# Down projection of a two-layer decoder trunk: seven products of half blocks in two phases

## The chip, the cores and the metric

One core of a Trainium2 chip runs the whole kernel. The metric is the device time of one execution in microseconds (us). TensorE (PE) multiplies, and PEld is its loading of the stationary operand; VectorE (DVE) and ScalarE (ACT) work element by element; GpSimd (POOL) does small steps and issues some transfers; SyncE (SP) issues most transfers. Sixteen DMA engines, shared by all queues, move the data.

## The reference

Two layers, each a token mixer and a gated feed-forward part with a short causal convolution, on 512 tokens of width 1024. The change lies in the last line of the feed-forward part:

```python
D_MODEL, SEQ, DEPTH, D_FF, FFN_CONV = 1024, 512, 2, 2816, 3

def conv_ffn(h, w_up, ffn_conv_w, w_down):
    u = causal_dwconv(h @ w_up, ffn_conv_w)
    gate, val = u[..., :D_FF], u[..., D_FF:]
    return (jax.nn.silu(gate) * val) @ w_down

for l in range(DEPTH):
    ...
    h = rmsnorm(x, g_pre_ffn[l])
    y = conv_ffn(h, w_up[l], ffn_conv_w[l], w_down[l])
    x = x + rmsnorm(y, g_post_ffn[l])
```

## The kernel before

**Arithmetic.** Every float32 operand of a large product is held as two tiles: a rounded part (format float32r) and the remainder. `mm3` (line 115) adds three products into one accumulator: rounded x rounded, rounded x remainder, remainder x rounded. `wsplit` (lines 99 to 108) loads a 512 KB weight tile `raw` over SyncE's queue (L102), ScalarE copies it into the rounded part (L105), VectorE subtracts that to get the remainder (L107). `split_evac` (L120, L121) does the same for a value on the chip.

**Up projection.** Lines 759 to 797 go over 22 pairs of channel blocks, gate block j = i and value block j = i + 22. Each block is 24 products of 512 tokens. `conv3` empties its accumulator: ScalarE takes one tap (L646), VectorE adds two (L648). Then comes the gate (L790, ScalarE), the product of the two (L791, VectorE), and the split into `G[0]` and `G[1]` (L120, L121), the transposed left side of the down projection: channels on the partitions, tokens along the tile, two blocks (k2) to a tile.

**Down projection.** Lines 800 to 832: 2816 channels are 22 blocks in 11 steps k2, the 1024 output columns two halves `hf`, the 512 tokens four row tiles `c`. For each half, step and row tile `down` does 2 x 3 products of 128 tokens by 512 columns. Half 0 adds up in four accumulators `acc`, half 1 in four `aux`. The weights of the last NTAIL = 5 steps of half 1 are made early and kept in the large pool `gp`, so that the end can go row tile by row tile: 30 products of tile c, then `postnorm` of c (square sums on ScalarE, L198; product with the gain, L200, and residual, L207, on VectorE; root on GpSimd, L203 and L204). Between the layers, `prenorm_a` of the next layer follows (L166, L175), `prenorm_b` transposes the result on TensorE (L183) and splits it (L188, L190), and `head` starts the next layer's products. After the last layer the rows go out (L209).

**Room and order.** `gp` has 21 tiles of 4 KB a partition, `wp` 6 for weights, `rp` 3 for raw tiles, `wk` 10 work tiles; each kind of accumulator has 4 banks. The program places instructions by dependencies, priority of program order and free tiles; a pool's tiles go to their first writers in program order. On the chip every engine and queue runs its own instructions strictly in that order and waits only on semaphores: where a load stands late in the program, it still starts as soon as its queue gets to it and its tile is free.

## Time and profile before

| | us |
|---|---|
| median of 3 runs (lowest, highest) | 1130.92 (1129.97, 1133.09) |
| the profiled execution | 1130.86 |
| its span, first to last instruction | 1129.1 |
| TensorE busy (products) | 1108.7, 98% |
| VectorE busy | 659.4, 58% |
| ScalarE busy | 455.9, 40% |
| DMA moved | 111.07 MB, mean 98 GB/s |

The profile is one execution. "Busy" is the time in which an engine had an instruction in work. Products overlap, so the mean time of one (0.389 us for 512 columns) is longer than the pace at which they follow each other; the pace is a stretch divided by its count. The layers' down projections lie at about 449 to 569 and 1007 to 1123 us. A wait is put down to what ended it last.

### The profile page before, as it was taken

What the parts mean: (1) busy time and instruction counts of PE and PEld (TensorE: products, weight loads), DVE (VectorE), ACT (ScalarE), POOL (GpSimd) and SP (SyncE); (2) the same over time, 40 slices, a digit from 0 to 9 for tenths busy, and PEclk for the clock granted to TensorE, in tenths of its full rate; (3) what the DMA queues carried; (4) which work ended last, traced back from release to release, by engine and by line L of the source; (5) the groups of instructions that cost most, each with busy time, mean ns of one, the idle gap of its engine ahead of it and who ended that gap; (6) DMA issues with size and microseconds to landing.
All of it is one profiled execution on the core that took longest, in us unless ns stands there. A gap on an engine that the chain in (4) does not pass through costs nothing.

```text
span 1129.1 us, 14371 instructions
## 1 busy us (share of the span) xinstructions
PE 1108.7 (98%) x5504; PEld 921.1 (82%) x5504; DVE 659.4 (58%) x1094; ACT 455.9 (40%) x882; POOL 46.7 (4%) x106
## 2 busy tenths in 40 slices
PE   6999999999999999999999999999999999999997
PEld 6877788988888888888897777889888888888886
DVE  5588775566666565223557887566566655652223
ACT  5454563444334443223354445444443334431221
POOL 2000011100000000000100000110000000000001
PEclk9999999999999999999999999999999999999999
DMA  7331440233333332334223215202222333233322
GB/s 265 110 98 45 145 135 13 89 112 93 95 101 104 93 93 93 98 108 127 81 93 107 77 62 187 75 19 90 98 94 93 96 102 102 94 93 93 97 90 74
DMA packets 33171, 111.07 MB, mean 98 GB/s; under 512 B 4192, under 2 KB 4352, under 8 KB 33104
## 3 DMA queue, kind: packets, MB, share of 16 engines
q1 hardware_dynamic: 29808, 102.98, 28.7%
q0 software_dynamic: 1232, 4.04, 1.1%
q10 hardware_dynamic: 2064, 3.15, 1.0%
q8 instruction: 43, 0.70, 0.3%
q14 instruction: 24, 0.20, 0.1%
HBM read 104.91 MB, written 2.10 MB: 95 GB/s over the span
## 4 chain that ended last, share of the span: by engine, by line
PE 91%; DVE 2%; DMA 1%; ACT 1%; issue 0%; ACTq 0%; DVEq 0%; POOLq 0%; POOL 0%
PE acc L115 74%; PE aux L115 11%; PE aux L513 1%; DMA wk<-wk 1%; PE aux L183 1%; PE aux L470 1%; PE aux L569 1%; PE aux L499 1%; PE aux L549 0%; DVE wk L412 0%; DVE w L107 0%; DMA raw<-in_wout_dram 0%; ACT wk L484 0%; PE aux L605 0%; PE aux L627 0%
## 5 line engine op out<-in xcount | busy, mean ns | idle before, releaser
L115 PE MATMUL acc<-g,w 128*128 128x512 f32 (+1 forms) x2256 | 482.0, 376 | 0.0
L115 PEld LDWEIGHTS acc<-g,w 128*128 128x128 f32 x2256 | 404.2, 188 | 76.7
L107 DVE TENSOR_TENSOR w<-raw,w 128x1024 fp32r<-128x1024 f32 (+2 forms) x162 | 192.8, 1191 | 267.6 <-ACT w L105 267.5
L105 ACT ACTIVATE w<-raw 128x1024 fp32r<-128x1024 f32 (+2 forms) x162 | 167.7, 1035 | 336.9 <-PE acc L115 294.7
L115 PE MATMUL acc<-w,h 128*128 128x384 f32 (+2 forms) x672 | 146.1, 364 | 0.7 <-DVE h L190 0.5
L648 DVE SCALAR_TENSOR_TENSOR wk<-acc,par,wk 128x511 f32<-128x511 f32 (+1 forms) x176 | 131.3, 746 | 3.0
L115 PEld LDWEIGHTS acc<-w,h 128*128 128x128 f32 x672 | 118.7, 190 | 17.2 <-issue 4.8
L115 PE MATMUL acc<-h,w 128*128 128x512 f32 x432 | 106.4, 398 | 0.0
L115 PEld LDWEIGHTS acc<-h,w 128*128 128x128 f32 x432 | 78.9, 188 | 18.2 <-issue 1.5
L115 PE MATMUL acc<-w,g 128*128 128x512 f32 x384 | 88.7, 389 | 0.0
L115 PEld LDWEIGHTS acc<-w,g 128*128 128x128 f32 x384 | 72.1, 188 | 15.0
L646 ACT ACTIVATE wk<-acc,par 128x512 f32<-128x512 f32 x88 | 58.9, 669 | 0.0
L115 PE MATMUL aux<-g,g 128*128 128x512 f32 x240 | 55.0, 389 | 0.0
L120 ACT ACTIVATE g<-wk 128x512 fp32r<-128x512 f32 x36 | 22.8, 633 | 76.3 <-DVE wk L791 68.3
L115 PEld LDWEIGHTS aux<-g,g 128*128 128x128 f32 x240 | 45.0, 188 | 9.3
L115 PE MATMUL acc<-h,g 128*128 128x512 f32 x192 | 45.2, 393 | 0.1
L115 PE MATMUL aux<-w,h 128*128 128x512 f32 x192 | 43.8, 389 | 0.0
L115 PEld LDWEIGHTS aux<-w,h 128*128 128x128 f32 x192 | 36.0, 188 | 7.5
L115 PEld LDWEIGHTS acc<-h,g 128*128 128x128 f32 x192 | 35.6, 188 | 7.7 <-ACT g L120 0.5
L175 DVE SCALAR_TENSOR_TENSOR wk<-x,rs,gb 128x512 f32<-128x512 f32 x32 | 22.7, 748 | 29.4 <-POOL rs L170 29.4
L203 POOL TENSOR_SCALAR rs<-ss 128x1 f32<-128x1 f32 x16 | 5.7, 358 | 747.0 <-ACT junk L198 747.0
L121 DVE TENSOR_TENSOR g<-wk,g 128x512 fp32r<-128x512 f32 x36 | 24.9, 690 | 18.6 <-ACT g L120 18.6
(172 smaller groups left out, 934.3 us busy)
## 6 DMA issues: line engine op xcount, KB each, us to landing
raw<-in_wup_dram SPq DMA_DIRECT2D x88, 512.0 KB, 3.5
raw<-in_wdn_dram SPq DMA_DIRECT2D x44, 512.0 KB, 3.5
raw<-in_wch_dram SPq DMA_DIRECT2D x18, 512.0 KB, 4.2
raw<-in_wout_dram SPq DMA_DIRECT2D x16, 512.0 KB, 3.6
raw<-in_wtb_dram SPq DMA_DIRECT2D x16, 384.0 KB, 3.0
raw<-in_wta_dram SPq DMA_DIRECT2D x8, 392.0 KB, 4.4
wk<-wk ACTq DMA_DIRECT2D x40, 64.0 KB, 2.1
x<-in_x_dram SPq DMA_DIRECT2D x4, 512.0 KB, 7.3
```

Source lines behind the costliest of these rows:

```text
L105: i = nc.scalar.activation(hi[:, :n], raw[:, :n], AF.Copy)
L107: after(nc.vector.tensor_tensor(lo[:, :n], raw[:, :n], hi[:, :n].bitcast(F32), ALU.subtract), gate2)
L115: i = nc.tensor.matmul(o, ls[a], rs[b], start=first and n == 0, stop=last and n == 2)
L120: i = nc.scalar.activation(hi, ps, AF.Copy)
L121: return i, nc.vector.tensor_tensor(lo, ps, hi.bitcast(F32), ALU.subtract)
L175: st[c] = nc.vector.scalar_tensor_tensor(h[:, :512], xs[c][:, sl], rs, gb[:, sl], ALU.mult, ALU.mult)
L183: nc.tensor.transpose(ps[:, k * 128:(k + 1) * 128], hs[hf][:, k * 128:(k + 1) * 128], ident)
L470: i = nc.tensor.matmul(pss[p][:, pr, k0:256], q[kv][r, qs], k[r, ks], start=n == 0, stop=n == 2)
L499: nc.tensor.transpose(ps[:, g * 128:(g + 1) * 128], t.P[:, g], ident)
L513: y.lastpv = nc.tensor.matmul(aos[k][64 * p:64 * p + 64, o:o + 256], y.avt[:, t.b - 1 + kh, t.kv * 64:t.kv * 64 + 64], t.PT[:, kh * 512 + ...
L646: nc.scalar.activation(u[:, :512], ps, AF.Copy, scale=cw[:, 2:3])
L648: nc.vector.scalar_tensor_tensor(u[:, d:512], ps[:, 0:512 - d], cw[:, 2 - d:3 - d], u[:, d:512], ALU.mult, ALU.add)
```

## The change

The down projection is seen as a product of 2 x 2 half blocks: the left side A has token halves (rows 0 to 255, 256 to 511) and even and odd channel blocks, the right side B has even and odd channel blocks and column halves. Instead of eight products of half blocks it uses seven, of sums of the blocks (Winograd's form). Per step k2 that is 7 products x 2 row tiles x 3 terms.

- `forms`, called once per pair of channel blocks in the up projection, makes the left sums on VectorE and splits them. Four left sides (products 1, 4, 5, 6) stay in `G`. Those of products 3 and 7 (tile X, 512 KB) and 2 (tile Y, 256 KB) are stored to DRAM by three transfers on GpSimd's queue.
- Phase one does products 1, 5, 6, 4 for all 11 steps, with all eight accumulators; a step loads two 512 KB weight tiles, makes three right sums (VectorE) and four splits. The last two steps are done together, product by product.
- Then three work tiles take combinations: `s1` = product 1, `sE` = product 5 less (1 + 6), `sF` = (1 + 6) + product 4.
- Phase two does products 2, 3, 7, with six accumulators. It loads the weights again (512 and 256 KB a step), makes one right sum and three splits, and loads X and Y back on GpSimd's queue. The last 4 steps are done row tile by row tile: row tiles 0 and 1 from products 2 and 3, row tiles 2 and 3 from product 7, with two more VectorE sums each before `postnorm`.

```diff
@@
-NTAIL = 5
+NTAIL = 4
@@
+    dp = ctx.enter_context(tc.tile_pool(name="dp", bufs=1, space=bass.MemoryType.DRAM))
@@
+    def forms(G, D7, k2, e, o):
+        for a in range(2):
+            G[a][k2] = slot(F32R, hp if k2 < 4 else gp)
+        g0, g1 = G[0][k2], G[1][k2]
+        a11, a21, a12, a22 = e[:, 0:256], e[:, 256:512], o[:, 0:256], o[:, 256:512]
+        t, u = work(), work()
+        nc.vector.tensor_tensor(t[:, 0:256], a21, a22, ALU.subtract)
+        nc.vector.tensor_tensor(t[:, 256:512], t[:, 0:256], a11, ALU.subtract)
+        nc.vector.tensor_tensor(u[:, 0:256], a12, t[:, 256:512], ALU.add)
+        nc.vector.tensor_tensor(u[:, 256:512], a11, a21, ALU.subtract)
+        split_evac(a11, g0[:, 0:256], g1[:, 0:256])
+        split_evac(a22, g0[:, 256:512], g1[:, 256:512])
+        _, last = split_evac(t[:, 0:512], g0[:, 512:1024], g1[:, 512:1024])
+        uh, ul, y = work(F32R), work(F32R), work(F32R)
+        split_evac(u[:, 0:512], uh[:, 0:512], ul[:, 0:512])
+        split_evac(a12, y[:, 0:256], y[:, 256:512])
+        D7[0][k2] = dp.tile([128, 1024], F32R, tag=f"dx{k2}", name=nm("dx"))
+        if k2 % 2 == 0:
+            D7[1][k2] = dp.tile([128, 1024 if k2 + 1 < NK2 else 512], F32R, tag=f"dy{k2}", name=nm("dy"))
+        else:
+            D7[1][k2] = D7[1][k2 - 1]
+        nc.gpsimd.dma_start(D7[0][k2][:, 0:512], uh[:, 0:512])
+        nc.gpsimd.dma_start(D7[0][k2][:, 512:1024], ul[:, 0:512])
+        nc.gpsimd.dma_start(D7[1][k2][:, (k2 % 2) * 512:(k2 % 2) * 512 + 512], y[:, 0:512])
+        return last
@@
-            k2 = i // 2
             if i % 2 == 0:
-                for a in range(2):
-                    G[a][k2] = slot(F32R, hp if k2 < 4 else gp)
-            o = [G[a][k2][:, (i % 2) * 512:(i % 2) * 512 + 512] for a in range(2)]
-            _, lastg = split_evac(s[:, :512], o[0], o[1])
+                ge = s
+            else:
+                lastg = forms(G, D7, i // 2, ge, s)
@@
-        banks = [[acc() for _ in range(NT)], None]
-
-        def down(hf, k2, w, c):
-            for kq in range(2):
-                k = 2 * k2 + kq
-                mm3(banks[hf][c], [G[a][k2][:, kq * 512 + c * 128:kq * 512 + c * 128 + 128] for a in range(2)],
-                    [w[a][:, kq * 512:kq * 512 + 512] for a in range(2)], k == 0, k == 2 * NK2 - 1)
-
-        for hf in range(2):
-            if hf:
-                banks[1] = [psum() for _ in range(NT)]
-            for k2 in range(NK2 - (NTAIL if hf else 0)):
-                w, _ = wsplit(wdn[l, hf, k2], 1024, wp)
-                for c in range(NT):
-                    down(hf, k2, w, c)
+        def raw(src, n=1024):
+            t = rp.tile([128, 1024], F32, tag="raw", name=nm("raw"))
+            nc.sync.dma_start(t[:, :n], src)
+            return t
+
+        def parts(src, pool):
+            w = slot(F32R, pool)
+            split_evac(src, w[:, 0:512], w[:, 512:1024])
+            return [w[:, a * 512:a * 512 + 512] for a in range(2)]
+
+        def add(p, q):
+            t = work()
+            nc.vector.tensor_tensor(t[:, :512], p, q, ALU.add)
+            return t[:, :512]
+
+        def left(n, k2, t):
+            if n in FA:
+                o = FA[n] * 256 + t * 128
+                return [G[a][k2][:, o:o + 128] for a in range(2)]
+            if n == 2:
+                o = (k2 % 2) * 512 + t * 128
+                return [Y[k2][:, o + a * 256:o + a * 256 + 128] for a in range(2)]
+            o = t * 128 + (256 if n == 7 else 0)
+            return [X[k2][:, o + a * 512:o + a * 512 + 128] for a in range(2)]
+
+        def prod(n, k2, t, w):
+            mm3(B[n][t], left(n, k2, t), w, k2 == 0, k2 == NK2 - 1)
+
+        FA = {1: 0, 4: 1, 5: 2, 6: 3}
+        X, Y, B = {}, {}, {}
+        for n in (1, 6, 5, 4):
+            B[n] = [psum() if n in (1, 6) else acc() for _ in range(2)]
+        ends = []
+        for k2 in range(NK2):
+            pool = wp if k2 < NK2 - 2 else gp
+            ra, rb = raw(wdn[l, 2 * k2]), raw(wdn[l, 2 * k2 + 1])
+            w = {1: parts(ra[:, 0:512], pool)}
+            t1 = add(ra[:, 0:512], ra[:, 512:1024])
+            w[5] = parts(t1, pool)
+            t2 = add(t1, rb[:, 512:1024])
+            w[6] = parts(t2, pool)
+            t4 = add(t2, rb[:, 0:512])
+            w[4] = parts(t4, pool)
+            if k2 < NK2 - 2:
+                for n in (1, 5, 6, 4):
+                    for t in range(2):
+                        prod(n, k2, t, w[n])
+            else:
+                ends.append((k2, w))
+        s1, sE, sF = slot(), slot(), slot()
+        for n in (1, 6, 5, 4):
+            for t in range(2):
+                for k2, w in ends:
+                    prod(n, k2, t, w[n])
+        us = []
+        for t in range(2):
+            nc.scalar.activation(s1[:, t * 512:t * 512 + 512], B[1][t], AF.Copy)
+        for t in range(2):
+            us.append(add(s1[:, t * 512:t * 512 + 512], B[6][t]))
+        for t in range(2):
+            nc.vector.tensor_tensor(sE[:, t * 512:t * 512 + 512], B[5][t], us[t], ALU.subtract)
+        for t in range(2):
+            nc.vector.tensor_tensor(sF[:, t * 512:t * 512 + 512], us[t], B[4][t], ALU.add)
+        B = {n: [psum() if n < 7 else acc() for _ in range(2)] for n in (2, 3, 7)}
         tail = []
-        for k2 in range(NK2 - NTAIL, NK2):
-            w, gate = wsplit(wdn[l, 1, k2], 1024, gp, lastg)
-            tail.append(w)
+        for k2 in range(NK2):
+            pool = wp if k2 < NK2 - NTAIL else gp
+            X[k2] = slot(F32R)
+            nc.gpsimd.dma_start(X[k2], D7[0][k2])
+            if k2 % 2 == 0:
+                Y[k2] = slot(F32R)
+                nc.gpsimd.dma_start(Y[k2][:, :1024 if k2 + 1 < NK2 else 512], D7[1][k2])
+            else:
+                Y[k2] = Y[k2 - 1]
+            rb, ra = raw(wdn[l, 2 * k2 + 1]), raw(wdn[l, 2 * k2][:, 512:1024], 512)
+            w = {2: parts(rb[:, 0:512], pool), 3: parts(rb[:, 512:1024], pool)}
+            w[7] = parts(add(ra[:, 0:512], rb[:, 512:1024]), pool)
+            if k2 < NK2 - NTAIL:
+                for n in (2, 3, 7):
+                    for t in range(2):
+                        prod(n, k2, t, w[n])
+            else:
+                tail.append((k2, w))
         more = l + 1 < L
         if more:
             hT = new_hT(hp)
-            y = start_layer(l + 1, gate)
+            y = start_layer(l + 1, None)
+
+        def comb(p, q, op):
+            t = work()
+            nc.vector.tensor_tensor(t[:, :512], p, q, op)
+            return t
+
         for c in range(NT):
-            for n, k2 in enumerate(range(NK2 - NTAIL, NK2)):
-                down(1, k2, tail[n], c)
+            t = c % 2
+            for n in ((2, 3) if c < 2 else (7,)):
+                for k2, w in tail:
+                    prod(n, k2, t, w[n])
             if more and c >= 2:
                 prenorm_b(c - 2, hs[c - 2], hT)
-            postnorm(c, banks[0][c], banks[1][c], gpost, None if more else out[c * 128:(c + 1) * 128, :])
+            sl = slice(t * 512, t * 512 + 512)
+            if c < 2:
+                p = comb(s1[:, sl], B[2][t], ALU.add), comb(sE[:, sl], B[3][t], ALU.add)
+            else:
+                p = comb(sF[:, sl], B[7][t], ALU.add), comb(sE[:, sl], B[7][t], ALU.subtract)
+            postnorm(c, *p, gpost, None if more else out[c * 128:(c + 1) * 128, :])
             if more:
                 hs[c] = prenorm_a(c, gpre)
@@
-    wdn = a["w_down"].reshape(L, 11, 2, 128, 2, 512).transpose(0, 4, 1, 3, 2, 5).reshape(L, 2, 11, 128, 1024)
+    wdn = a["w_down"].reshape(L, 22, 128, 1024)
```

## Rows read from the trace of the kernel before

**Rows 1.** The page: busy us of each engine (share of the span) xinstructions.

```profile
PE 1108.7 (98%) x5504; PEld 921.1 (82%) x5504; DVE 659.4 (58%) x1094; ACT 455.9 (40%) x882; POOL 46.7 (4%) x106
```

**Rows 2.** The chain of waits: start us, us, engine, tile, line.

```profile
768.64 294.42 PE acc L115 x1344
1063.06 59.85 PE aux L115 x264
```

**Rows 3.** Busy by stretch: PE, PEld, DVE, ACT, POOL, PEclk, DMA share, GB/s.

```profile
5.00:10.00 5.00, 0.97 (x5) 0.97 (x6) 2.01 (x4) 2.01 (x3) 0.79 (x2) 1.00 1.01 386
10.00:15.00 5.00, 4.85 (x17) 3.85 (x15) 3.52 (x7) 4.13 (x9) 1.20 (x3) 1.00 0.82 310
300.00:400.00 100.00, 100.00 (x443) 82.84 (x442) 61.14 (x74) 41.08 (x56) 0.00 (x0) 1.00 0.31 99
460.00:500.00 40.00, 40.00 (x178) 33.14 (x177) 9.80 (x8) 7.68 (x8) 0.00 (x0) 1.00 0.29 92
900.00:1000.00 100.00, 100.00 (x443) 82.81 (x442) 60.68 (x74) 41.12 (x56) 0.00 (x0) 1.00 0.31 95
```

**Rows 4.** Instructions by shape, 331 to 460 us: busy us, mean ns, idle before.

```profile
L115 PEld LDWEIGHTS acc<-g,w 128*128 128x128 f32 x517 | 97.1, 188 | 20.1
...
L121 DVE TENSOR_TENSOR g<-wk,g 128x512 fp32r<-128x512 f32 x12 | 8.3, 692 | 7.7 <-ACT g L120 7.7
L120 ACT ACTIVATE g<-wk 128x512 fp32r<-128x512 f32 x12 | 7.6, 632 | 29.3 <-DVE wk L791 29.3
```

**Rows 5.** The same view, VectorE, 545 to 600 us.

```profile
L190 DVE TENSOR_TENSOR h<-aux,h 128x256 fp32r<-128x256 f32 x16 | 5.8, 415 | 0.4 <-ACT h L188 0.4
...
L207 DVE SCALAR_TENSOR_TENSOR x<-wk,rs,x 128x512 f32<-128x512 f32 x8 | 5.6, 745 | 0.3 <-POOL rs L204 0.3
```

**Rows 6.** DMA queues and issues: transfers, KB each, median us to landing.

```profile
q1 hardware_dynamic: 29808, 102.98, 28.7%
...
raw<-in_wdn_dram SPq DMA_DIRECT2D x44, 512.0 KB, 3.5
...
gb<-in_gv_dram POOLq DMA_DIRECT2D x3, 512.0 KB, 4.2
```

**Rows 7.** The timeline, end of the first up projection: start us, us, instruction.

```profile
449.41 1.23 DVE L107 TENSOR_TENSOR w<-raw,w 128x1024 fp32r<-128x1024 f32 x1 [2.17 <-ACT w L105]
...
450.55 1.53 DVE L648 SCALAR_TENSOR_TENSOR wk<-acc,par,wk 128x511 f32<-128x511 f32 x2
452.18 0.69 DVE L791 TENSOR_TENSOR wk<-wk,wk 128x512 f32<-128x512 f32 x1
...
453.57 0.69 DVE L121 TENSOR_TENSOR g<-wk,g 128x512 fp32r<-128x512 f32 x1 [0.70 <-ACT g L120]
```

**Rows 8.** The timeline, one gate product and its split.

```profile
419.54 0.69 DVE L791 TENSOR_TENSOR wk<-wk,wk 128x512 f32<-128x512 f32 x1
420.27 0.63 ACT L120 ACTIVATE g<-wk 128x512 fp32r<-128x512 f32 x1 [2.44 <-DVE wk L791]
420.94 0.69 DVE L121 TENSOR_TENSOR g<-wk,g 128x512 fp32r<-128x512 f32 x1 [0.70 <-ACT g L120]
```

**Rows 9.** The timeline of GpSimd, first layer: a vector's load.

```profile
213.44 0.61 POOL L158 DMA_DIRECT2D gb<-in_gv_dram  x1 [1.75 <-DVE wk L175]
```

**Rows 10.** The timeline, end of the first layer.

```profile
562.02 7.06 PE L115 MATMUL aux<-g,g 128*128 128x512 f32 x30
...
577.06 1.42 DVE L175 SCALAR_TENSOR_TENSOR wk<-x,rs,gb 128x512 f32<-128x512 f32 x2 [2.02 <-POOL rs L170]
...
579.25 1.04 PE L183 MATMUL aux<-cs,wk 128*128 128x128 f32 x8
```

**Rows 11.** The timeline, last row tile of the kernel.

```profile
1122.93 0.60 ACT L198 ACTIVATE junk<-aux 128x512 bf16<-128x512 f32 x1 [5.54 <-PE aux L115]
...
1124.70 1.41 DVE L207 SCALAR_TENSOR_TENSOR x<-wk,rs,x 128x512 f32<-128x512 f32 x2 [0.35 <-POOL rs L204]
```

More of the change, by code (lines that the diff above doesn't have):

```diff
@@ L759, in tile_hymba_trunk @@
         G = [[None] * NK2 for _ in range(2)]
+        D7 = [[None] * NK2, [None] * NK2]
         first = {}
```

## The prediction

> **What bounds the kernel now.** I read the busy table first: TensorE is busy in 98% of the span, VectorE in 58%, ScalarE in 40% [rows 1]. Busy alone doesn't prove a bound, so the chain of waits comes second: it runs through TensorE's products almost without a break, and its longest links are 294 and 60 us of products of line 115, back to back, through the up projection, the down projection and the end of the second layer [rows 2]. Third, the table by stretches gives the pace at the granted clock of 1.00 (the 2.4 GHz level): 443 products in 100 us, 0.2257 us each, the same in both up projections; the down projection has 178 in 40 us, 0.225 us [rows 3]. There VectorE is busy in a quarter of the time and the DMA engines at 0.29, 92 GB/s. So in the part that changes, a product taken away is worth its 0.2257 us as long as VectorE, ScalarE and the transfers still deliver in time. The profiled execution took 1130.86 us, its span 1129.1, so 1.8 lie around it; the median is 1130.92, 0.06 away. The sum is made against 1130.9. A measurement can tell 0.3%, 3.4 us, from no change.
>
> **What is removed.** Before, a layer's down projection is 2 halves x 22 blocks x 4 row tiles x 3 split terms = 528 products of 512 columns. After, it is 7 x 11 x 2 x 3 = 462, of the same shape. Two layers save 132; 132 x 0.2257 = **29.8 us**.
>
> **Up projection: the left sums.** For each pair of channel blocks (96 products, 21.7 us) two splits of 512 columns on VectorE, 2 x 0.69 [rows 4], give way to four sums and three splits of 256 columns and two splits of 512. A 256-column step takes 0.415 us [rows 5], so 7 x 0.415 + 2 x 0.69 = 4.3 us against 1.4: 2.9 us more in 21.7, VectorE from 61% [rows 3] to about 75%. The cover is four accumulators and three pairs of weight tiles, which let VectorE lag by two products' groups, some 11 us, and the new burst is 4.3 us. I cost it at 0; without cover it would be 2.9 x 11, 32 us a layer. Three stores of 256 KB per pair go out from GpSimd's queue, 36 GB/s on top of 99 [rows 3]. Nobody waits for them until the second phase, except that the ten work tiles are held until a store has landed; the nearest transfer on that queue, 512 KB, takes 4.2 us to landing [rows 6], against 21.7 between bursts: 0.
>
> **Start of phase one.** Before, the last channel's tail on VectorE is taps, gate product, split, up to about 454.3 [rows 7], while TensorE already multiplies by weights made earlier. After, the 0.69 us split is 4.3 us of sums, and the second step's weights (four splits, three sums, 7 x 0.69 = 4.8 us) queue behind or beside them. TensorE finishes the first step 24 x 0.2257 = 5.4 us after the up projection's end. If the sums go first, the first weight is some 3.3 us late, if they interleave, 0. I take 1 us a layer, nearer to 0 because the rows show VectorE taking weight splits between the taps [rows 7]: **2 us**.
>
> **Phase one, steady.** A step is 24 products, 5.42 us. VectorE has 7 x 0.69 = 4.84 us, ScalarE 4 x 0.63 = 2.5 us [rows 4]: both fit, VectorE narrowly. But each sum goes VectorE to ScalarE (rounded part) and back (remainder). The trace has that handover: the gate product starts at 419.54, ScalarE's copy 0.73 us later, VectorE's remainder 0.67 us after that, VectorE idle for 0.70 [rows 8]. If other steps fill the gap it costs nothing, if they never do, 13 us a layer (worked out as a rival below). The work is independent (next sums, next step's first split), so I take 0.5 a layer: **1 us**. A step reads 1.05 MB in 5.42 us, 193 GB/s. A 512 KB tile lands 3.5 us after issue [rows 6] and three buffers allow 1.57 MB per 8.1 us at just that demand: 0.
>
> **Phase two: the transfers.** This is the step I trust least. A step is 18 products, 4.07 us, but it reads 0.786 MB of weights again and 0.786 MB on average of the stored sums: 386 GB/s if all came in time with the products. It needn't: a slot for the stored tiles comes free as phase one uses up the left tiles of step 6 and later, and the loads stand in GpSimd's queue behind nothing that is late (its other loads, 512 KB vectors, go out hundreds of microseconds before [rows 9]). Count from the last two steps of phase one, which are done together: 48 products, 10.8 us, then seven steps, 28.4 us, and about 2 us into the last four: 41 us. Still to come then: 8 x 0.524 of X, 2.36 of Y, 11 x 0.786 of weights, 15.2 MB. Two rates from the trace bracket that. The only stretch with all DMA engines occupied moved 386 GB/s [rows 3]: 39.4 us, no stall. The main queue's total, 102.98 MB in 28.7% of the span [rows 6], is 318 GB/s: 47.8 us, 7 us late. I take 1.5 a layer, nearest to the stretch in which the queues were really full: **3 us**. VectorE (4 x 0.69 = 2.8 us a step) is no limit here.
> The rows reach 386 GB/s; the Trainium skill (HBM Reference, Specifications (TRN2)) puts the effective rate of one core at about 358 GB/s. By that figure, an estimate, the 15.2 MB would take 42.5 us, 1.5 us late a layer; by the row nothing would be late.
>
> **Between the phases.** Eight accumulators give way to six. One copy on ScalarE and the sums on VectorE read each bank as its last product ends, while 36, 24 and 12 products of the others (8.1 to 2.7 us) still run: 0, bounds 0 to 2 us if the last two reads are waited for.
>
> **The end of layer one.** The four row tiles ended 30 products, 6.8 us, apart [rows 10]; now the first two take 24 and the last two 12 products, 2.7 us. Each has two sums more (1.4 us on VectorE), in all 4 x 0.69 + 4 x 0.745 = 5.7 us of VectorE. Before, the last tile's norm ends on VectorE at 578.48 and TensorE transposes it at 579.25 [rows 10]: 0.8 us to spare. Now its chain is 1.4 us longer and queues 3.0 us (5.7 less 2.7) behind the tile before it: 1.4 + 3.0 - 0.8 = **3.6 us**; bounds 0 (the next layer's other products go first) and 6 (all four tiles' 22.8 us and 6.6 us of transposed splits in a row, from 11.9 us before the products' end to 17.5 after, where TensorE would be there at about 11.4).
>
> **The end of the kernel.** From the last product to the end it is 6.2 us now (1122.93 [rows 11] to 1129.1). Two sums come in front and the tile before is only 2.7 us ahead: bounds 0 and 3, I take **1.5 us**.
>
> **The sum.** 1130.9 - 29.8 + 2 + 1 + 3 + 3.6 + 1.5 = 1112.2: **1112 us**, faster by 1.7%.
>
> **The rivals.**
> *Slower: the handover between VectorE and ScalarE sets phase one's pace.* If VectorE's queue holds each remainder right behind its sum, a step is three times sum to copy, copy to remainder, remainder (0.73 + 0.67 + 0.6 = 2.0 us) plus the first split, 0.6: 6.6 us for 5.42 of products; 1.2 x 11 x 2 = 26 us, less the 1 already counted: **1137 us**. It decides as soon as more than one of the three gaps stays unfilled. For it: in the up projection that gap does stay empty [rows 8]. Against it: there nothing else was ready.
> *Faster, but less: the transfers bound phase two.* At 318 GB/s the 7 us a layer replace 1.5: 1112 + 11 = **1123 us**; at 310, the next densest stretch [rows 3], 1125. Against it: the demand is spread over two queues that were never full together. For it: the stored tiles are in the rounded format, and no transfer of the trace writes that format.
> The Trainium skill (DMA: Bandwidth & Descriptors, SWDGE vs HWDGE vs iDMA) says that a DMA into a float32r destination always casts and must be issued from GpSimd. It gives no rate for that, and no run here shows one, so it moves no number here.
> *Slower, by the stored tiles:* if transfers in the rounded format held the DMA engines twice as long as others, the 6.55 MB of X and Y would count as 13.1, in all 21.75 MB, 56.3 us at 386 GB/s, 15.3 late: 1112 + 2 x 13.8 = **1140 us**. Against it: a plain 512 KB load on that queue lands in 4.2 us, hardly later than the 3.5 of the main queue [rows 6].
> *Everything is hidden:* only the two ends cost, 1130.9 - 29.8 + 2.5 = **1104 us**.
> *It doesn't do what it says:* fewer products, but each slower. The stationary loads take 0.188 us under 0.226 [rows 4] and the shapes don't change; I give it nothing of its own.
>
> **How the numbers follow.** The forecast, 1106 to 1118: 0.58. All hidden, below 1106: 0.10. The transfers, 1118 to 1127.5: 0.13. Cases mixed, within 3.4 us of before: 0.05. Slower by the handover: 0.07; slower by the stored tiles: 0.07. So faster 0.81, same 0.05, slower 0.14. The range, 1104 to 1134, leaves out about 0.06 below and 0.14 above.
>
> **What would show it.** The product count of line 115 should fall by 132 and the pace in the new stretch stay at 0.226 us. In phase one, VectorE should be busy in about 85 to 90% with TensorE gapless; gaps there named after VectorE's remainders mean the first rival. In phase two the DMA share should be near 1.0 at the start and 350 GB/s or more; idle TensorE named after a raw or a stored tile means the second. At the layer's end a gap of some 4 us should stand before the third or fourth transpose. The prediction falls if the up projection slows at all, since 32 us a layer of VectorE work lie there behind cover.

## The result and the profile after

The changed kernel takes **1169.01 us** (median of 4 runs, 1162.75 to 1171.63) against 1130.75 for the kernel before (now also 4 runs): 1.0327 times as long, 95% interval 1.0282 to 1.0372. I had forecast 1112, in a range of 1104 to 1134. The sign was wrong. The profiled execution took 1171.63 us, its span 1169.9, 40.8 more than the span before.

The page of the changed kernel has these lines on engines and DMA queues (beside [rows 1] and [rows 6]; columns: busy us, share, instructions; queue, packets, MB, share of 16 engines):

```profile
PE 1102.2 (94%) x5372; PEld 908.0 (78%) x5372; DVE 826.3 (71%) x1474; ACT 526.3 (45%) x1062; POOL 100.5 (9%) x206
...
q1 hardware_dynamic: 36144, 120.28, 32.3%
q0 software_dynamic: 15632, 38.65, 10.2%
```

The 132 products are gone (5504 less 5372), as the change says. But TensorE's busy time fell by 6.5 us only, since part of the rest ran at the lower clock (the granted clock is 0.973 over the span, 0.999 before), and its share fell from 98% to 94%. Where, the table by stretches of the changed kernel shows (columns as in [rows 3]: PE, PEld, DVE, ACT, POOL, PEclk, DMA share, GB/s):

```profile
300.00:400.00 100.00, 100.00 (x443) 82.81 (x442) 73.82 (x111) 44.65 (x69) 7.95 (x15) 1.00 0.46 136
455.00:460.00 5.00, 1.76 (x4) 1.13 (x5) 4.94 (x9) 2.84 (x6) 1.59 (x3) 0.50 0.58 142
460.00:465.00 5.00, 5.00 (x14) 3.92 (x13) 4.96 (x10) 3.00 (x6) 0.00 (x0) 0.56 0.97 330
465.00:500.00 35.00, 35.00 (x156) 28.98 (x155) 29.41 (x49) 16.50 (x28) 1.07 (x2) 1.00 0.60 198
500.00:520.00 20.00, 19.70 (x87) 15.99 (x86) 16.38 (x28) 8.98 (x17) 5.30 (x10) 1.00 1.08 396
520.00:540.00 20.00, 14.99 (x55) 11.37 (x54) 6.82 (x11) 4.61 (x8) 1.60 (x3) 0.83 0.80 275
580.00:600.00 20.00, 13.93 (x64) 12.93 (x64) 15.50 (x28) 8.94 (x27) 3.65 (x8) 0.73 0.09 27
```

The up projection (first line) and the steady part of phase one (465 to 500) run gapless at the old pace. Time goes in three places: between the up projection and phase one (455 to 465), in phase two (520 to 540), and in the norms at the layer's end (580 to 600). In all three the granted clock is low as well.

**Place A, the start of phase one.** In the kernel before, TensorE goes over into the down projection without a wait:

```profile
448.34 21.92 PE L115 MATMUL acc<-w,h 128*128 128x512 f32 x96
```

The timeline of the changed kernel, VectorE and TensorE (start us, us, instruction, the idle time before it and what ended it):

```profile
453.43 0.42 DVE L662 TENSOR_TENSOR wk<-wk,wk 128x256 f32<-128x256 f32 x1
...
455.89 1.03 DVE L122 TENSOR_TENSOR wk<-wk,wk 128x512 fp32r<-128x512 f32 x2
456.84 0.68 DVE L843 TENSOR_TENSOR wk<-raw 128x512 f32<-128x512 f32 x1
457.56 0.69 DVE L843 TENSOR_TENSOR wk<-wk,raw 128x512 f32<-128x512 f32 x1
```
```profile
450.15 1.52 PE L116 MATMUL aux<-w,h 128*128 128x512 f32 x6
458.24 3.23 PE L116 MATMUL acc<-w,h 128*128 128x512 f32 x6 [6.57 <-ACT w L121]
```

The first right sum (line 843) begins only at 456.84, behind the whole of the last pair's left sums and their splits (453.43 to 456.9). Of the first step's four weights only the one that is no sum was ready: six products at 450.15, then 6.57 us of nothing.

**Place B, phase two.** GpSimd's issues of the stored tiles, VectorE and TensorE in the changed kernel:

```profile
498.34 0.54 POOL L899 DMA_DIRECT2D g<-dx  x1 [40.41 <-PE acc L116]
...
520.71 0.53 POOL L899 DMA_DIRECT2D g<-dx  x1 [1.96 <-PE acc L116]
```
```profile
530.84 0.69 DVE L843 TENSOR_TENSOR wk<-raw,raw 128x512 f32<-128x512 f32 x1 [4.33 <-DMA raw<-in_wdn_dram]
...
535.24 0.69 DVE L843 TENSOR_TENSOR wk<-raw,raw 128x512 f32<-128x512 f32 x1 [3.11 <-DMA raw<-in_wdn_dram]
```
```profile
532.19 2.55 PE L116 MATMUL aux<-w,g 128*128 128x512 f32 x6 [3.17 <-DVE w L122]
536.59 2.50 PE L116 MATMUL aux<-w,g 128*128 128x512 f32 x5 [1.85 <-DVE w L122]
```

The time from issue to landing of the raw weights (tile `raw`, 515 to 545 us):

```profile
DMA to landing us min/median/max: 2.5/3.6/9.5
```

The stored tiles wait for slots until 498 and are then issued in a heap, 14 loads up to 521.8. The DMA engines are full (396 GB/s), and the raw weights behind which the next products stand come late, up to 9.5 us after their issue.

**Place C, the norms.** VectorE in the changed kernel at the end of layer one (lines 921: the two combining sums of a row tile; 176: its norm for the next layer; 108: a weight split of the next layer):

```profile
566.15 0.98 DVE L108 TENSOR_TENSOR w<-raw,w 128x784 fp32r<-128x784 f32 x1 [1.89 <-ACT w L106]
...
567.65 1.28 DVE L921 TENSOR_TENSOR wk<-g,aux 128x512 f32<-128x512 f32 x2
...
577.37 1.42 DVE L176 SCALAR_TENSOR_TENSOR wk<-x,rs,gb 128x512 f32<-128x512 f32 x2 [2.32 <-POOL rs L171]
578.70 1.28 DVE L921 TENSOR_TENSOR wk<-g,aux 128x512 f32<-128x512 f32 x2
...
588.26 1.27 DVE L921 TENSOR_TENSOR wk<-g,acc 128x512 f32<-128x512 f32 x2
...
596.90 1.28 DVE L921 TENSOR_TENSOR wk<-g,acc 128x512 f32<-128x512 f32 x2
```

The first row tile's sums stand behind a weight split of the next layer. Each later row tile's sums start only when the tile before has been through its whole chain, waits for ScalarE and GpSimd included: 11.1, 9.6 and 8.6 us apart, although all products were done at 574.9. The stretch from the last product to the end of the next layer's heads (the first products of that layer, `head`), after and before:

```profile
569.29 5.60 PE L116 MATMUL acc<-g,g 128*128 128x512 f32 x24
...
611.73 2.30 PE L116 MATMUL acc<-g,h 128*128 128x392 f32 x12
```
```profile
562.02 7.06 PE L115 MATMUL aux<-g,g 128*128 128x512 f32 x30
...
586.54 2.30 PE L115 MATMUL acc<-g,h 128*128 128x392 f32 x12
```

What each place costs is read from TensorE's timeline: the length of a stretch, less its products times the pace of 0.2267 us (six in 1.36 us in phase one).

| place | forecast | layer one | layer two |
|---|---|---|---|
| A: start of phase one | 2 | 9.9 | 9.7 |
| B: last two steps of phase one, phase two, its tail | 3 | 10.2 | 15.1 |
| C: layer's end (39.14 us from last product to the heads' end, before 19.76); kernel's end (12.9, before 6.2) | 3.6 and 1.5 | 19.4 | 6.7 |
| all | 10.1 | 39.5 | 31.5 |

71.0 - 29.8 = 41.2, against 40.8 more in the span (the 1 us forecast for steady phase one didn't show). So the gain was real, and 71 us were lost around it.

### The profile page after: what moved, and what is told of

Read it like the earlier page. It is cut to its first block, busy times and chain, and to the rows that moved or that the text cites. A ratio compares the mean times of both kernels' runs of the same rounds, so it can differ in the third digit from the quotient of the medians.

```text
span 1169.9 us, 15146 instructions
## 1 busy us (share of the span) xinstructions
PE 1102.2 (94%) x5372; PEld 908.0 (78%) x5372; DVE 826.3 (71%) x1474; ACT 526.3 (45%) x1062; POOL 100.5 (9%) x206
## 3 DMA queue, kind: packets, MB, share of 16 engines
q1 hardware_dynamic: 36144, 120.28, 32.3%
q0 software_dynamic: 15632, 38.65, 10.2%
## 4 chain that ended last, share of the span: by engine, by line
PE 36%; DMA 5%; DVE 5%; ACT 2%; issue 1%; POOL 1%; DVEq 0%; POOLq 0%; ACTq 0%; SPq 0%
PE acc L116 32%; DMA raw<-in_wdn_dram 5%; DVE wk L843 1%; PE aux L116 1%; ACT junk L199 1%; DVE w L122 1%; PE aux L184 1%; PE aux L514 1%; DVE w L108 0%; PE aux L471 0%; ACT wk L485 0%; DVE x L208 0%; DMA raw<-in_wout_dram 0%; DVE g L122 0%; POOL rs L205 0%
## 5 line engine op out<-in xcount | busy, mean ns | idle before, releaser
L108 DVE TENSOR_TENSOR w<-raw,w 128x1024 fp32r<-128x1024 f32 (+2 forms) x128 | 151.1, 1182 | 113.5 <-ACT w L106 113.5
L106 ACT ACTIVATE w<-raw 128x1024 fp32r<-128x1024 f32 (+2 forms) x128 | 131.7, 1029 | 191.4 <-PE acc L116 180.3
L649 DVE SCALAR_TENSOR_TENSOR wk<-acc,par,wk 128x511 f32<-128x511 f32 (+1 forms) x176 | 131.3, 746 | 15.9 <-ACT wk L647 13.0
L116 PE MATMUL aux<-w,g 128*128 128x512 f32 x288 | 74.1, 401 | 9.4 <-DVE w L122 9.4
L121 ACT ACTIVATE g<-wk 128x512 fp32r<-128x512 f32 (+1 forms) x70 | 37.8, 543 | 94.4 <-DVE wk L822 66.0
L116 PEld LDWEIGHTS aux<-w,g 128*128 128x128 f32 x288 | 55.1, 193 | 22.9 <-DVE w L122 11.4
L121 ACT ACTIVATE w<-wk 128x512 fp32r<-128x512 f32 x68 | 42.6, 631 | 66.6 <-DVE wk L843 44.0
L647 ACT ACTIVATE wk<-acc,par 128x512 f32<-128x512 f32 x88 | 59.0, 670 | 12.7 <-PE acc L116 12.7
L116 PE MATMUL acc<-g,g 128*128 128x512 f32 x240 | 57.5, 394 | 0.0
L116 PEld LDWEIGHTS acc<-g,g 128*128 128x128 f32 x240 | 45.3, 190 | 9.4
L122 DVE TENSOR_TENSOR g<-wk,g 128x512 fp32r<-128x512 f32 (+1 forms) x70 | 40.4, 580 | 11.2 <-ACT g L121 11.2
L122 DVE TENSOR_TENSOR w<-wk,w 128x512 fp32r<-128x512 f32 x68 | 45.4, 685 | 2.6 <-ACT w L121 2.4
```

The lines of the kernel that those rows point to most:

```text
L106: i = nc.scalar.activation(hi[:, :n], raw[:, :n], AF.Copy)
L108: after(nc.vector.tensor_tensor(lo[:, :n], raw[:, :n], hi[:, :n].bitcast(F32), ALU.subtract), gate2)
L116: i = nc.tensor.matmul(o, ls[a], rs[b], start=first and n == 0, stop=last and n == 2)
L121: i = nc.scalar.activation(hi, ps, AF.Copy)
L122: return i, nc.vector.tensor_tensor(lo, ps, hi.bitcast(F32), ALU.subtract)
L647: nc.scalar.activation(u[:, :512], ps, AF.Copy, scale=cw[:, 2:3])
```

## The experiments

Theory: A, B and C are three separate losses, A and C made by the order in which work is queued on VectorE, B by transfers that come in a heap, and each is made larger by the clock that falls behind a wait. Rivals: VectorE simply has too much to do, whatever the order; phase two is slow by its handovers; the low clock has another cause. Where stretches are compared below, they are from these profiled runs (us):

| kernel | median | ratio to before (95%) | to last product, layer one | from there to heads' end | to last product, layer two | to the end |
|---|---|---|---|---|---|---|
| before | 1130.75 | | 569.1 | 19.8 | 534.1 | 6.2 |
| after | 1169.01 | 1.028 to 1.037 | 574.9 | 39.1 | 543.0 | 12.9 |
| first sums early | 1153.45 | 1.017 to 1.021 | 569.7 | 36.1 | 534.6 | 12.9 |
| norms interleaved | 1161.31 | 1.024 to 1.030 | 572.9 | 33.4 | 537.8 | 12.7 |
| no reload | 1144.34 | 1.009 to 1.014 | 572.8 | 31.3 | 530.6 | 11.4 |
| first two together | 1147.85 | 1.012 to 1.016 | 567.3 | 34.7 | 532.0 | 12.6 |
| earlier slots | 1162.42 | 1.025 to 1.032 | 573.4 | 36.3 | 538.1 | 12.9 |
| three edits | 1145.07 | 1.010 to 1.014 | 567.0 | 32.2 | 531.1 | 12.5 |
| and split norm | 1140.11 | 1.006 to 1.009 | 568.0 | 30.7 | 530.9 | 10.7 |
| and deeper loads | 1136.29 | 1.001 to 1.005 | 566.6 | 30.4 | 530.2 | 10.0 |
| split norm and new order of the tail | 1143.95 | 1.006 to 1.012 | 568.0 | 32.7 | 532.0 | 10.7 |
| deeper loads and new order | 1139.01 | 1.004 to 1.009 | 565.5 | 32.7 | 529.9 | 9.5 |
| the same, tail of three | 1136.82 | 1.002 to 1.005 | 563.8 | 34.7 | 528.1 | 11.1 |
| wait put into before | 1147.51 | 1.012 to 1.015 | 577.5 | 19.8 | 542.6 | 6.2 |

**The first step's sums early.** The raw loads and the three sums of step 0 (`sums`) are written ahead of the last pair, behind the loads and splits of that pair's own up weights (`late`):

```diff
         for i in range(2 * NK2):
             us = []
+            if i == 2 * NK2 - 1:
+                late = {j: upw(j) for j in (i, i + 2 * NK2)}
+                early = sums(0)
             for j in (i, i + 2 * NK2):
...
-                    w = upw(j)
+                    w = late[j] if i == 2 * NK2 - 1 else upw(j)
...
+            if k2 == 0:
+                w = {n: parts(p, pool) for n, p in zip((1, 5, 6, 4), early)}
```

> The raw loads and the three sums of the first step of phase one stand ahead of the last pair's taps and forms on VectorE; everything else is as in the changed kernel. Theory (the start of phase one is lost to the place of the sums): TensorE's 6.6 us wait at the first step goes, and with it the 5 us in which its products ran at half the clock behind that wait; the changed kernel lost 9.9 and 9.7 us there in its two layers, so the time falls by 15 to 20 us, to 1149 to 1154 us, if the last pair's own work, moved back by three sums, isn't itself late. Rival (VectorE simply has too much to do at this place, whatever the order): another wait of the same kind takes its place, on the forms' last splits, and the time falls by under 5 us, to 1164 to 1169.

Measured: 1153.45, 15.6 us less. In the profile of this kernel (VectorE, TensorE, then the stretch, columns as in [rows 3]):

```profile
440.61 0.68 DVE L816 TENSOR_TENSOR wk<-raw 128x512 f32<-128x512 f32 x1
...
457.99 1.92 PE L116 MATMUL acc<-w,h 128*128 128x512 f32 x6 [1.45 <-ACT w L121]
...
455.00:460.00 5.00, 3.56 (x15) 2.31 (x14) 4.96 (x9) 2.82 (x6) 1.58 (x3) 1.00 0.61 133
```

The sums now stand between the taps, at 440.61. The wait of 6.57 us has become one of 1.45, before the second step, whose sums still follow the forms, and the clock stays at 1.00. VectorE has the same work and is as full (4.96 of 5 us). So A is mostly the place of the sums, not the amount of work: 2.0 of its 9.9 us in layer one are left. The three places aren't quite apart, though: in layer one phase two, which now comes earlier, loses 13.4 us instead of 10.2.

**The norms interleaved.** At the end of layer one, row tile c's norm for the next layer is written behind tile c+1's second norm:

```diff
-            if more:
-                hs[c] = prenorm_a(c, gpre)
+            if more and c:
+                hs[c - 1] = prenorm_a(c - 1, gpre)
         if more:
+            hs[3] = prenorm_a(3, gpre)
```

> At the end of layer one the first norm of the next layer is put for each row tile behind the second norm of the row tile after it; nothing else is changed, the end of the kernel included. Theory (the four row tiles' norm chains run one behind the other, 9.4 us each, because each chain's ScalarE and VectorE work is queued whole ahead of the next combine): the 39.0 us from the last product of phase two to the heads' end falls towards the 19.6 us of the kernel before; 8 to 15 us less, so 1154 to 1161. Rival (the chains are as long as their own arithmetic and the order between them is free): under 3 us, 1166 to 1169.

Measured: 1161.31, 7.7 us less, a little under the theory's span, far over the rival's. The stretch from last product to heads' end fell from 39.1 to 33.4 us, and the combining sums stand 7.3 to 7.7 us apart instead of 8.6 to 11.1. Between the first and the last of them VectorE is now busy in 19.5 of 22.6 us, in the changed kernel in 22.1 of 29.3. So the order was part of C; but with the better order VectorE is nearly full there, and what remains may well be the rival, too much work for VectorE.

**No reload.** Phase two reads back only the first step's stored tiles and uses them in all steps:

```diff
-            X[k2] = slot(F32R)
-            nc.gpsimd.dma_start(X[k2], D7[0][k2])
...
+            if k2 == 0:
+                X[k2], Y[k2] = slot(F32R), slot(F32R)
+                nc.gpsimd.dma_start(X[k2], D7[0][k2])
+                nc.gpsimd.dma_start(Y[k2], D7[1][k2])
+            else:
+                X[k2], Y[k2] = X[0], Y[0]
```

> The sums of the left side are still made and stored, but in phase two only the first step's three tiles are read back and used in all eleven steps: 10 of 11 of those loads are left out, and the output is another one. Products, weights and their sums are the same in number. Theory (phase two and the end of phase one lose their time to transfers: the reloads run ahead on their own queue at 390 to 410 GB/s and the raw weights land up to 9.5 us late): most of the 25 us lost in the two phase twos goes, 15 to 25 us less, 1144 to 1154. Rival (phase two is slow by its handover from VectorE and ScalarE to TensorE and the slow clock, not by transfers): under 5 us less, 1164 to 1169.

Measured: 1144.34, 24.7 us less, the upper end of the theory. The stretches of this kernel, and the one longer wait of TensorE that is left in its first phase two:

```profile
500.00:520.00 20.00, 20.00 (x90) 16.57 (x89) 17.20 (x29) 8.55 (x16) 0.00 (x0) 1.00 0.64 223
520.00:540.00 20.00, 19.77 (x87) 15.95 (x87) 12.44 (x21) 9.48 (x15) 0.00 (x0) 1.00 0.55 198
...
554.93 10.31 PE L116 MATMUL aux<-g,g 128*128 128x512 f32 x37 [2.37 <-ACT g L121]
```

Without the loads phase two is gapless until the tail (87 products in 20 us against 55), with all its handovers: the gap there is made by the loads. The edit takes away two things at once, their bytes and the slots that they hold, and doesn't tell these apart; that in the changed kernel the wait before the gap's sums is for the raw weights' DMA (530.84, 535.24) speaks for the bytes. What the tail's weights cost stays (the last line). In layer one only 2.1 us of the gain show up to the last product and 7.8 in the stretch behind it, where the next layer's first transposes now run among the last products; layer two gains 12.4 in the products.

**Both changes of order.**

> The two changes of order together: the first step's sums ahead of the last pair's taps, and the norms of neighbouring row tiles interleaved at the end of layer one. If the losses are separate, the two gains add: 23 to 35 us less than the changed kernel, 1134 to 1146 us, about the time of the kernel before. If one of them only shifts the wait to the other, the sum is clearly less than the two single gains.

Measured: 1147.85, 21.2 us less, against 23.3 for the two single gains, and just short of the 23 to 35 expected: separate losses, near enough. The norms' edit takes off 5.6 us here, with intervals that are apart (1.0124 to 1.0161 against 1.0170 to 1.0209); alone, its interval and the changed kernel's overlap.

**Earlier slots for the reloads.** The same bytes, another time:

```diff
-            X[k2] = slot(F32R)
+            X[k2] = slot(F32R, hp if k2 < 4 else gp)
...
-                Y[k2] = slot(F32R)
+                Y[k2] = slot(F32R, hp if k2 < 4 else gp)
```

> One edit to the changed kernel: the stored tiles that phase two reads back for its first four steps go into the eight slots of the pool that the first four steps of phase one leave free, instead of the pool of 21 that the right weights of the last steps and the three sums also want. The bytes are the same. Theory (the reloads come in a heap, eleven tiles between 490 and 513 us, because their slots come free late, and hold up the raw weights there): the loads start some 20 us earlier, the stretch from 500 to 520 us falls from 390 GB/s to under 330, and the time falls by 10 to 20 us, to 1148 to 1158. Rival (the bytes of phase two as such, whenever they come): within 5 us of the changed kernel, 1163 to 1169.

Measured: 1162.42, 6.6 us less by the medians: between the two. The intervals of both kernels overlap (1.0254 to 1.0315 and 1.0282 to 1.0372), so the size of this gain is open. This kernel's stretches, GpSimd's first load, and TensorE:

```profile
500.00:520.00 20.00, 17.06 (x64) 12.63 (x63) 15.46 (x26) 8.51 (x15) 2.55 (x5) 0.91 0.88 311
520.00:540.00 20.00, 20.00 (x90) 16.56 (x89) 14.27 (x23) 8.54 (x15) 1.17 (x3) 1.00 0.77 250
...
464.09 0.54 POOL L899 DMA_DIRECT2D h<-dx  x1 [6.85 <-PE acc L116]
...
511.55 0.50 PE L116 MATMUL aux<-g,g 128*128 128x512 f32 x1 [1.90 <-ACT g L121]
```

The loads start 34 us earlier (464 instead of 498), the rate from 500 to 520 falls from 396 to 311 GB/s, and from 520 to 540 the products are gapless. So it was the time of the loads, the heap, that made the gap there. But TensorE's wait for the split weights of phase one's last two steps, 0.30 us in the first layer of the changed kernel, is now 1.90 and 0.77, and the clock there 0.91.

**The three edits together.**

> All three edits: first sums ahead of the last pair's taps, norms of neighbouring row tiles interleaved at the end of layer one, and the reloads of the first four steps into the earlier slots. If the three losses are separate, this is the time of the two edits of order together, 1147.9, less what the earlier slots give alone: 1128 to 1138 us, about the kernel before or just under it. If the earlier slots only move the wait to the tail's weights, it stays above 1142.

Measured: 1145.07, only 2.8 us under the two edits of order, where 6.6 would have been the sum. I had hoped for the kernel before's time. TensorE's waits at the start of phase two (2.10 and 0.78 us in layer one with the two edits) are gone, but a new one stands in the third step of phase one, 1.83 us in layer one and 2.34 in layer two:

```profile
468.29 2.32 PE L116 MATMUL aux<-w,h 128*128 128x512 f32 x5 [1.83 <-DVE w L122]
```

There VectorE waits for raw weights (1.59 us), and the DMA engines are full (409 GB/s from 465 to 470). So the earlier slots mostly move the wait: the stored tiles now meet the raw weights of phase one.

**The norm cut in two.** On top of the three edits, a row tile's last multiply-add follows the next tile's sums and squares:

```diff
-            postnorm(c, *p, gpost, None if more else out[c * 128:(c + 1) * 128, :])
...
+            post[c] = postnorm_a(c, *p, gpost)
+            if c:
+                finish(c - 1)
+        finish(3)
```

> As the kernel with three edits, but the norm behind phase two is cut in two for each row tile: the sums, squares and the mean of row tile c+1 are put ahead of the last multiply-add of row tile c, in both layers. Theory (the four row tiles' chains run one behind the other at the kernel's end too, 12.9 us from the last product against 6.2): the kernel's end shortens by 4 to 6 us, and the end of layer one by a few more; 5 to 10 us less than the kernel with three edits. Rival (the end is the arithmetic of one row tile): under 2 us less.

Measured: 1140.11, 5.0 us less by the medians, just under the low end of the theory; the profiled spans differ by 2.5. The kernel's end shortens by 1.8 us instead of 4 to 6, the layer's end by 1.5.

**Deeper loads, the tail's order, a shorter tail.** Three more, on top of that kernel. Deeper loads (the half tile of raw weights goes to a work tile):

```diff
-            rb, ra = raw(wdn[l, 2 * k2 + 1]), raw(wdn[l, 2 * k2][:, 512:1024], 512)
+            rb, ra = raw(wdn[l, 2 * k2 + 1]), work()
+            nc.sync.dma_start(ra[:, 0:512], wdn[l, 2 * k2][:, 512:1024])
```

> The kernel with three edits and the split norm (1140.1 us), and one thing more: in phase two the half of a raw weight tile that each step loads goes into a work tile of its own, so that the three raw buffers hold three steps' loads instead of one and a half. Theory (what is left of phase two's loss is the short lead of the raw loads: TensorE waits 2 to 3 us a layer for the tail's weights and runs at half the clock behind that wait): 4 to 8 us less, 1132 to 1136. Rival (the lead is set by the slots of the split weights, not by the raw buffers): within 2 us, 1138 to 1142.

The tail's order (`for i, c in enumerate((0, 2, 1, 3))` instead of `for c in range(NT)`):

> The kernel with three edits and the split norm (1140.1 us), with the tail's row tiles in the order 0, 2, 1, 3: a row tile of 24 products, one of 12, one of 24, one of 12, instead of the two of 12 last. Theory (the last two row tiles' products end 2.7 us apart, while a row tile's norm needs 4 us and more of VectorE, so that their norms queue at the end): 3 to 6 us less over both ends, 1134 to 1137. Rival (the tail is held by its weights, and using the seventh product's weights earlier only makes TensorE wait for them): no gain or a loss, 1139 to 1145.

Both:

> The deeper loads and the tail's new order together. If both theories hold, the gains add, 7 to 14 us: 1126 to 1133, faster than the kernel before (1131.8) or level with it. If the lead of the weights is the one cause, it is the time of the deeper loads alone.

Both, with `NTAIL = 3`:

> As the last, with three steps instead of four kept for the tail, so that fewer split weights must be ready at once and less time is left to cover the norms. Theory (the tail waits for weights): 2 to 4 us less than with four steps. Rival (the norms are what the tail must cover; 12 products fewer stand beside them): 2 to 5 us more than with four steps.

Measured: 1136.29 (1.0013 to 1.0053), 1143.95 (1.0058 to 1.0117), 1139.01 (1.0038 to 1.0092) and 1136.82 (1.0021 to 1.0052). The deeper loads give 3.8 us, just short of the theory's 4 to 8. The new order is 3.8 us slower by the medians, with intervals that overlap, and tells little; with the deeper loads it missed the 1126 to 1133 expected: in TensorE's queue the seventh product's matmuls for row tile 2 stand among those of row tile 1 (in ones to fives, from 555.45 to 562.39) and not ahead of them, so that the order written is not the order run; and both it and the kernel without it wait in the first tail for the first row tile's weights (1.80 and 1.65 us, against 2.36), not for the seventh's, so its rival isn't shown either. Three steps instead of four may give 2 us; the intervals overlap, so that is open. None beats the kernel before.

**The wait alone.** What a wait costs was measured in the kernel before, with one VectorE addition a layer and nothing else changed:

```diff
         nc.sync.dma_start(raw[:, :n], src)
+        if late is not None:
+            nc.vector.scalar_tensor_tensor(raw[:, 0:512], late, 0.0, raw[:, 0:512], ALU.mult, ALU.add)
...
-                w, _ = wsplit(wdn[l, hf, k2], 1024, wp)
+                w, _ = wsplit(wdn[l, hf, k2], 1024, wp, late=None if hf or k2 else s[:, :512])
```

> The kernel before the change, with one wait put in and no work taken out or moved: the raw weights of the first step of the down projection are added, on VectorE, to nought times the last gate product of the up projection, so that their split can begin only when that product is there (some 453 us), as the sums of the changed kernel have to wait; one addition of 0.7 us a layer. TensorE should then wait 5 to 8 us, in one or two pieces, between the up and the down projection of each layer. Theory (a wait of this length costs more than itself, since the granted clock falls to half behind it: 9.9 us were lost to 6.6 us of waiting in the changed kernel): the time lost in each layer is 1.3 to 1.6 times the wait, 14 to 22 us in all, 1146 to 1154, and the profile shows the low clock in the 5 to 10 us behind the wait. Rival (the clock was low in the changed kernel for another reason, such as its many waits before): the loss is the wait alone, 10 to 15 us in all, 1142 to 1147, at a clock of 1.00 throughout.

Measured: 1147.51 against 1131.64 on the same chip, 15.9 us more. The profile of this kernel, TensorE and the stretches:

```profile
453.73 21.54 PE L117 MATMUL acc<-w,h 128*128 128x512 f32 x81 [4.96 <-ACT w L107]
...
450.00:455.00 5.00, 1.24 (x3) 0.52 (x3) 4.37 (x7) 3.03 (x5) 0.00 (x0) 0.76 0.01 3
455.00:460.00 5.00, 5.00 (x13) 3.95 (x14) 2.20 (x2) 0.57 (x1) 0.00 (x0) 0.55 0.76 217
460.00:465.00 5.00, 5.00 (x24) 4.14 (x23) 1.23 (x1) 1.06 (x1) 0.00 (x0) 1.00 0.25 98
```

TensorE waits 4.96 us in each layer. Behind the wait 13 products take the 5 us in which 24 do at the full clock, at a granted clock of 0.55, near half of 2.4 GHz. The products lose 8.4 us in layer one and 8.5 in layer two: 1.7 times the wait, somewhat over the theory's 1.6 (by the medians it is 8.0 a layer, 1.6). The rival, a clock at 1.00, falls. The changed kernel's start of phase one is this case: 6.57 us of waiting, 9.9 lost.

## Why the prediction was wrong

**The gain** (29.8 us): right. 132 products are gone and the pace in phase one is 0.2267 us, the same as in the timeline of the kernel before (96 products in 21.76 us); my 0.2257 came from counting a stretch.

**The up projection** (0): right. 443 products in 100 us as in [rows 3], VectorE at 74%; I had said 75.

**The start of phase one** (2 us; measured 19.6). The step that failed is "TensorE finishes the first step 24 x 0.2257 = 5.4 us after the up projection's end". It took the first step's four weights as made beforehand and let only the second step's queue. Three of the four are sums, and they stand behind the left sums in VectorE's queue: cover was one weight's six products, 1.4 us, not 5.4. My "3.3 us late" as an upper bound fell with it. [rows 7] showed weight splits between the taps, but of weights whose place in the program was there already; a row that shows work between the taps doesn't show that new work would be put there. Putting the sums there by hand gave back 15.6 us.

**Phase one, steady** (1 us; none measured): right, and the first rival with it refuted: gapless from 465 to 500, VectorE at 84%. The handover's gap of 0.70 us [rows 8] was filled by other work.

**Phase two** (3 us; measured 25.3 with the last two steps of phase one and the tail). The rate was right: the rows of the changed kernel reach 396 GB/s where I had counted on 386. The step that failed is the sum itself, "15.2 MB" divided by a rate against 41 us: it asks whether all bytes come in time and not whether the right ones come first. Fourteen loads of stored tiles, some of them for the tail, which starts 36 us later, went ahead of raw weights needed at once; later, with the heap through, the engines were not full (275 GB/s from 520 to 540), probably because three raw buffers keep only so many loads under way (the deeper loads took off 3.8 us), so the lost time didn't come back. Leaving out the loads took 24.7 us away, with which this is shown for the loads as a whole, their slots included; that the heap is what matters is shown for the gap at 520 to 540 (earlier slots), while the time of the whole kernel fell by 6.6 only, and in the kernel with three edits the same collision came back in phase one. The sign that I had named for the second rival, the transfers, did come (DMA share 1.08, TensorE idle behind raw weights); but it too went by the mean rate, and its 7 us a layer were too few (10.2 and 15.1, the tail and the clock included).
The Trainium skill (HBM Reference, Specifications (TRN2)) has about 358 GB/s as a core's share when both cores of a pair stream, and about 425 for a core that streams alone. The changed kernel, on one core, moved 396 over 20 us, which lies between the two; the 358 in my prediction was the share of two streaming cores. Neither figure would have found the loss: it was one of order.

**The rival of the stored tiles** is refuted by the page: the queue with the rounded format moved 38.65 MB in 10.2% of the engines' time, 324 GB/s for a full share, and the main queue 120.28 in 32.3%, 318. So the rounded format cost the engines nothing more here.
The Trainium skill (DMA: Bandwidth & Descriptors, SWDGE vs HWDGE vs iDMA) says that a float32r destination, the rounded format of this kernel, always casts and must be issued from GpSimd; what it costs it doesn't say, and by these two rates it is no more than a plain load.

**The two ends** (5.1 us; measured 26.1). The step that failed is "1.4 + 3.0 - 0.8": it let the last row tile queue behind one tile only, and at VectorE's busy time. The work of a tile was right (5.7 us forecast, about 5.5 measured). But a tile's chain is queued whole before the next tile's sums, so the four run one behind the other from the first on, 11.1, 9.6 and 8.6 us apart: beside its 5.5 us for the chain VectorE spends 1 to 3 on the next layer's weight and transposed splits, and is idle for 1.9 to 3.2, waiting for ScalarE and GpSimd. Before, 30 products, 6.8 us, lay between two row tiles; now it is 24 and at the end 12. That part of my argument was right, and its price five times too low. Order gave back some of it: with interleaved and split norms the stretch at the layer's end is 30.7 us and the kernel's end 10.7, still 10.9 and 4.5 more than before; with VectorE nearly full there, I don't know how much of this another order could still take away.

**The clock** was in no term. A stall was costed at its length; behind the stall of 5 us it was worth 1.6 to 1.7 times that.

**What is left of it.** The best version with all products and loads is still 1.0033 (1.0013 to 1.0053) of the kernel before. Its span, 1137.2, lies 37.9 us over the old one less 29.8. By the table: 10.6 at the layer's end, 3.8 at the kernel's, 12.4 and 11.0 in the two layers' products. Two waits of TensorE in the first steps of phase one (1.44 and 1.85 us in layer one, 1.45 and 2.63 in layer two, the larger ones in the third step, where the reloads now run) are part of it, and behind the last of them the clock is 0.50 from 1030 to 1035. In its tail two more waits show (TensorE, then the stretch, columns as in [rows 3]):

```profile
549.53 0.50 PE L116 MATMUL aux<-g,g 128*128 128x512 f32 x1 [1.54 <-ACT g L121]
...
551.39 9.76 PE L116 MATMUL aux<-g,g 128*128 128x512 f32 x29 [1.36 <-DVE g L122]
...
550.00:560.00 10.00, 8.64 (x26) 6.85 (x26) 7.08 (x11) 4.47 (x9) 1.16 (x2) 0.66 0.51 173
```

They are 1.54 and 1.36 us, for the tail's split weights, and the clock is 0.66 in the 10 us from 550. The change takes work from TensorE alone and gives VectorE more, 826 us for 659; at the starts and ends of the stages VectorE's sums, splits and norms now stand on the path. Whether another arrangement of the tail would bring the rest is open; of those tried, a new order of its row tiles didn't run as written and a shorter tail was within the scatter.

## What to carry to other kernels

A product taken away is worth its pace only where its weights are ready: at each start of a new stage, count for the first step, weight by weight, what stands ahead of it in the queue of the engine that makes it. Ask of transfers not only whether the bytes fit but which are issued first when slots come free in a heap, and, before moving loads to slots that come free earlier, what they meet there. Cost a chain over several engines by its whole length, handovers and the other work in the same queue included, and ask how many such chains stand one behind the other. Cost a TensorE stall of some 5 us, in a kernel like this one, at half as much again.

## What the runs showed of the hardware

- A wait of 4.96 us on TensorE put into a kernel that otherwise ran at a clock of 1.00 was followed by 5 us at 0.55; one of 1.45 us, in the kernel with the early sums, by no fall (1.00 in its 5 us stretch). Two of 1.54 and 1.36 us within 2 us of each other (the kernel with the deeper loads) went with 0.66 in the 10 us from 550, a stretch that begins between them.
- Both DMA queues together moved 396 GB/s over 20 us (500 to 520 in the changed kernel). Over the whole span the rounded-format queue moved as much for a full share of the engines as the plain one (324 and 318 GB/s).
- In the same kernel the raw weights issued from 515 to 545 us landed up to 9.5 us after their issue; the median was 3.6.
